# Attention beside a projection: V's first half turned sooner, a head's end in two steps

## The chip, the cores and the metric

The kernel runs on one core of one Trainium2 chip. The metric is the device time of one execution in microseconds. Five engines work side by side, each through its own instructions in the order in which the program lists them: TensorE (PE; its weight loads are shown as PEld), VectorE (DVE), ScalarE (ACT), GpSimd (POOL) and SyncE (SP), which here issues the transfers. An instruction that waits for a semaphore holds up all that stand behind it on its engine.

## The reference

One layer of a hybrid decoder on a sequence of 1024 tokens of width 2048, in float32. Cut to what matters here:

```python
proj = x @ w_in        # split: q, k, v, g_att (8 heads x 128 each), fg, conv and pool parts
cum = cumsum(log_sigmoid(fg + b_f))            # per head
logits = q @ k.T * 128 ** -0.5 + cum[q] - cum[k]      # causal: k <= q
y_att = softmax(logits) @ v * silu(g_att)
y = concat([y_att, y_conv, y_pool])            # each with its own silu gate
x = layer_norm(2 ** 0.25 * x + y @ w_out)
```

## The kernel before

A float32 product is made as three matmuls of a high and a low half (`mm3`): each operand is split by ACT, which casts the high half (L121), and DVE, which subtracts to get the low half (L122). Weights go through this under the names wr (as loaded) and wh (split), tiles of the softmax under t and pt, V under v, Q and K under qk.

The program has a first and a second pass over the input projection and then the output projection. In the second pass, 28 pairs of column blocks are projected in turn (8 `mm3` per block half and product); all that isn't projection runs beside it. It is put into slots of a queue: `at(slot, step)` adds a step some slots ahead, and every third `mm3` of the projection calls `tick()`, which takes the next slot and runs its steps. So a slot lasts about 2 to 2.6 us.

`attention(h, ...)` puts one head into these slots. Its 1024 queries are treated as two halves, n=0 (4 blocks of 128 keys) and n=1 (8 blocks), all tiles being keys x queries: `scores(n, j)` in slots 3 to 6 and 7 to 14; `find_top(n)` behind them, the maximum over the keys; `shift` (adds the negated maximum, L759), `probs` (exponential, on ACT L765), `parts` (the split into pt) and `values` (the product with V into the bank o) at slot e0 + j and one to three later, with e0 = 12 and 20; `turn_v(n)` transposes one half of V (PE, L675) and splits it; `invert(n)` makes the reciprocals of the row sums; `finish(n)` weights o with the gate (L797), multiplies by the reciprocals (L798), and stores the result. Behind `finish(1)`, `sums_of_y` loads, adds and stores sums of the results for the output projection (POOL and SP). A maximum or a row sum goes from one row to all 128 partitions through DRAM: `to_all` transposes a small tile on DVE (L745), writes it (m_dram) and reads it back to all partitions (the tile mb). Both the shift and L798 wait for such an mb.

What sets the order is not the slots alone. The steps are traced slot by slot, which gives each instruction its rank; a list scheduler then lays the instructions of each engine by rank and by when its model of the chip takes their inputs to be ready, and what it makes is the fixed order of the engine. The shift alone is held to the order of tracing: `keep_in_program_order` pins it behind the DVE instruction that was traced last before it. Buffers come from rings by tag: `gate` (tiles pa and pb, tag "pc", 7 buffers) is the gate that L797 and L798 overwrite with the result, and its buffer serves a later pair of blocks once the stores and `sums_of_y` have read it.

Of the kernel before, what the change touches and what calls it, by code (L numbers as in the profile page):

```python
# [36 lines left out]
ALU = mybir.AluOpType  # L37
# [8 lines left out]
H = S // 2  # L46
# [27 lines left out]
def layer(ctx: ExitStack, tc: tile.TileContext, xt, x, wp, wf, b_f, conv_w, pool_w, pool_scale,  # L74
          w_out, ln_g, ln_b, out):
    nc = tc.nc
# [31 lines left out]
    def hl(name, tag):  # L108
        return tile_of([P, 2, H], F32R, name, tag)
# [7 lines left out]
    def bank(tag):  # L117
        return ps.tile([P, 512], F32, tag=tag, bufs=4, name=nm(tag))

    def split(hi, lo, src):  # L120
        nc.scalar.copy(hi, src)  # L121
        nc.vector.tensor_tensor(lo, src, hi.bitcast(F32), ALU.subtract)  # L122
# [43 lines left out]
    def at(slot, step):  # L166

        while len(side) <= slot:
            side.append([])
        side[slot].append(step)  # L170
# [481 lines left out]
    def store_y(e, y, n):  # L652
        nc.sync.dma_start(y_dram[e, n], y[:, n * H : n * H + H])
# [13 lines left out]
    def attention(h, qs, ks, vt, gate):  # L667
        t, pt, v, o, top, down, total = {}, {}, {}, {}, {}, {}, {}

        def turn_v(n):  # L670
            def go():
                acc, th = bank("aux"), hl("v", "v")
                for a in range(4):
                    c = (n * 4 + a) * P
                    nc.tensor.transpose(acc[:, a * P : a * P + P], vt[:, c : c + P], ident)  # L675
                split(th[:, 0], th[:, 1], acc)
                v[n] = th
            return go
# [4 lines left out]
        def scores(n, j):  # L683
            def go():
                tj, c0 = half("t", "t"), first(n, j)
                t[n, j] = tj
                cw = min(c0, 256)
                if cw < c0:
                    nc.gpsimd.memset(tj[:, cw:c0], 0.0)
                acc = bank("aux")  # L690
                js = slice(j % 4 * P, j % 4 * P + P)
                kj = ks[j // 4]
                mm3(acc[:, cw:], kj[:, 0, js], kj[:, 1, js], qs[n][:, 0, cw:], qs[n][:, 1, cw:], True, True)
                ck = ncum[:, h, j : j + 1]
                plain = c0
                if j >= 4 * n:
                    plain = c0 + P
                    nc.vector.scalar_tensor_tensor(tj[:, c0:plain], acc[:, c0:plain], ck, mask, ALU.add, ALU.add)
                if plain < H:
                    nc.scalar.activation(tj[:, plain:H], acc[:, plain:], AF.Identity, bias=ck)  # L700
                if j:
                    fold_max(n, j, acc, ck, plain)
            return go
# [47 lines left out]
        def find_top(n):  # L751
            def go():
                down[n] = to_all(across(top[n], ALU.max), h * 4 + n)
            return go

        def shift(n, j):
            def go():
                tj, c0 = t[n, j], first(n, j)
                tc.keep_in_program_order(nc.vector.tensor_tensor(tj[:, c0:], tj[:, c0:], down[n][:, c0:], ALU.add))  # L759
            return go  # L760

        def probs(n, j):
            def go():
                tj, c0 = t[n, j], first(n, j)
                nc.scalar.activation(tj[:, c0:], tj[:, c0:], AF.Exp)  # L765
                if j:
                    fold(total, n, j, ALU.add, nc.gpsimd)
            return go

        def parts(n, j):  # L770
            def go():
                cw, th = min(first(n, j), 256), hl("pt", "pt")
                split(th[:, 0, cw:], th[:, 1, cw:], t[n, j][:, cw:])
                pt[n, j] = th
            return go

        def values(n, j):
            def go():
                if j == 0:
                    o[n] = bank("aux")  # L780
                cw = min(first(n, j), 256)
                js = slice(j % 4 * P, j % 4 * P + P)
                vj, th = v[j // 4], pt.pop((n, j))
                mm3(o[n][:, cw:], vj[:, 0, js], vj[:, 1, js], th[:, 0, cw:], th[:, 1, cw:], j == 0, j == 4 * n + 3)
            return go

        def invert(n):
            def go():
                w = across(total[n], ALU.add)
                nc.vector.reciprocal(w[:, :16], w[:, :16])  # L790
                total[n] = to_all(w, h * 4 + 2 + n)
            return go

        def finish(n):
            def go():
                y = gate[:, n * H : n * H + H]
                nc.vector.tensor_tensor(y, o[n], y, ALU.mult)  # L797
                nc.vector.tensor_tensor(y, y, total[n], ALU.mult)  # L798
                store_y(h, gate, n)
                if n:  # L800
                    at(1, sums_of_y(h, gate))
            return go

        for n, s0, e0 in ((0, 3, 12), (1, 7, 20)):
            js = 4 * n + 4
            for j in range(js):
                at(s0 + j, scores(n, j))
                at(e0 + j, shift(n, j))
                at(e0 + j + 1, probs(n, j))
            for j in range(js):  # L810
                at(e0 + j + 2, parts(n, j))
                at(e0 + j + 3, values(n, j))
            at(s0 + js, find_top(n))
            at((4, 9)[n], turn_v(n))
            at(e0 + js + 2, invert(n))
            at(e0 + js + 7, finish(n))


    def pool_steps(g, u, gate):
# [55 lines left out]
    def sums_of_y(k, y):  # L875
        def go():
            a21, s3 = half("a21", "m"), half("s3y", "m")
            nc.sync.dma_start(a21, y_dram[KH + k, 1])
            nc.sync.dma_start(s3, sy_dram[2, k])
            nc.gpsimd.tensor_tensor(s3, y[:, H:], s3, ALU.subtract)  # L880
            nc.sync.dma_start(sy_dram[1, k], s3)
            nc.gpsimd.tensor_tensor(a21, y[:, H:], a21, ALU.add)
            nc.sync.dma_start(sy_dram[0, k], a21)
            nc.gpsimd.tensor_tensor(y[:, :H], y[:, :H], s3, ALU.subtract)
            nc.sync.dma_start(sy_dram[3, k], y[:, :H])
        return go
# [48 lines left out]
    def use(role, g, a, b):  # L935
        if role == "vg":
            held[g] = a, b
        elif role == "qk":
            attention(g, *held.pop(("qk", g)), *held.pop(g))
        elif role == "pool":  # L940
            pool_steps(g, b, silu(a))
        elif role == "conv":
            held["conv"] = conv_steps(g, a, b)
        else:
            conv_gate(g, held.pop("conv"), a, b)
# [340 lines left out]
```

## Time and profile before

| | |
|---|---|
| median of 3 runs | 1631.89 us (1631.51 to 1632.08) |
| the profiled execution | 1629.22 us |
| its span, first to last instruction | 1627.5 us |
| granted TensorE clock, mean | 0.989 |
| busy: PE / PEld / DVE / ACT / POOL | 95% / 77% / 69% / 43% / 23% |
| first start of L798, last start | 750.3 us, 1360.5 us |
| heads 0 to 7 begin (first transpose of V) | 701, 781, 864, 951, 1037, 1128, 1201, 1276 us |

In a row of the timeline the columns are the start in us, the duration in us, the engine, the line, the operation, the tile written and the tiles read, the shape, and how many instructions the row holds; in square brackets, the engine's idle time before it and what ended that. A row of the waits holds the engine, line and tile that waited, what it waited for, the total in us, how often, and the longest.

### The profile page before, as it was taken

To read this page: it belongs to the slowest core of one execution; us is meant where nothing else is said; L and a number is where in the kernel's file an instruction comes from. 1 tells how busy PE (TensorE), PEld (TensorE's weight loads), DVE (VectorE), ACT (ScalarE), POOL (GpSimd) and SP (SyncE) were. 2 spreads that over 40 slices of the span, in tenths; PEclk is the share of its full clock that TensorE was granted. 3 is DMA by queue.
4 is the path that set the end of the run, shared out by engine and by line. 5 is a ranking of instruction groups with operands and counts; after the bars stand their busy time and mean duration, and the time that the engine had idled before them with its cause. 6 is when DMAs were issued, how large, how long until landed. Compare 5 with 4: busy or idle time off the path is not lost. (4 is left out here: it accounts for less than half of the span.)

```text
span 1627.5 us, 20130 instructions
## 1 busy us (share of the span) xinstructions
PE 1553.6 (95%) x6812; PEld 1254.3 (77%) x6812; DVE 1129.3 (69%) x1659; ACT 691.9 (43%) x1238; POOL 381.5 (23%) x303
## 2 busy tenths in 40 slices
PE   8999999999999999999999999999988998999986
PEld 6887888778787787788878777867766777788775
DVE  6754676666665656378787868577779875566797
ACT  4421221211121225566665656575666553444420
POOL 0232232222222220012232323343326322100000
PEclk9999999999999999999999999999999999999998
DMA  8756988887878667534545454535344445657572
GB/s 253 263 205 210 323 292 296 304 305 255 289 266 293 241 241 253 212 133 157 183 154 185 149 181 156 172 126 196 132 146 161 153 140 205 193 174 228 193 233 104
DMA packets 156807, 339.92 MB, mean 209 GB/s; under 512 B 17952, under 2 KB 27040, under 8 KB 156704
## 3 DMA queue, kind: packets, MB, share of 16 engines
q1 hardware_dynamic: 156704, 338.64, 61.2%
q8 instruction: 53, 0.87, 0.2%
q14 instruction: 50, 0.41, 0.1%
HBM read 247.28 MB, written 91.29 MB: 208 GB/s over the span
## 5 line engine op out<-in xcount | busy, mean ns | idle before, releaser
L122 DVE TENSOR_TENSOR wh<-wr,wh 128x512 fp32r<-128x512 f32 x264 | 199.4, 761 | 92.4 <-ACT wh L121 91.8
L121 ACT CAST wop<-wb 128x1024 fp32r<-128x1024 f32 x76 | 80.0, 1053 | 319.3 <-PE aux L129 139.2
L121 ACT CAST wh<-wr 128x512 fp32r<-128x512 f32 x264 | 161.5, 618 | 83.6 <-PE acc L130 27.9
L128 PE MATMUL acc<-x,wh 128*128 128x512 f32 x448 | 178.6, 399 | 3.3 <-ACT wh L121 3.3
L130 PE MATMUL acc<-x,wh 128*128 128x512 f32 x448 | 178.0, 397 | 3.4 <-DVE wh L122 3.4
L130 PE MATMUL aux<-xs,wop 128*128 128x512 f32 x448 | 175.5, 392 | 3.5 <-DVE wop L122 3.4
L129 PE MATMUL acc<-x,wh 128*128 128x512 f32 x448 | 176.3, 394 | 0.0
L128 PE MATMUL aux<-xs,wop 128*128 128x512 f32 x448 | 174.6, 390 | 0.0
L129 PE MATMUL aux<-xs,wop 128*128 128x512 f32 x448 | 174.4, 389 | 0.0
L122 DVE TENSOR_TENSOR wop<-wb,wop 128x1024 fp32r<-128x1024 f32 x76 | 102.7, 1352 | 27.1 <-ACT wop L121 27.0
L130 PEld LDWEIGHTS acc<-x,wh 128*128 128x128 f32 x448 | 84.7, 189 | 28.6 <-DVE wh L122 10.7
L130 PEld LDWEIGHTS aux<-xs,wop 128*128 128x128 f32 x448 | 84.1, 188 | 25.2 <-DVE wop L122 7.6
L128 PEld LDWEIGHTS acc<-x,wh 128*128 128x128 f32 x448 | 84.9, 190 | 22.5 <-ACT wh L121 7.2
L129 PEld LDWEIGHTS aux<-xs,wop 128*128 128x128 f32 x448 | 84.1, 188 | 17.7
L128 PEld LDWEIGHTS aux<-xs,wop 128*128 128x128 f32 x448 | 84.1, 188 | 17.5
L129 PEld LDWEIGHTS acc<-x,wh 128*128 128x128 f32 x448 | 85.0, 190 | 15.7
L130 PE MATMUL acc<-xs,wh 128*128 128x512 f32 x224 | 87.8, 392 | 3.4 <-DVE wh L122 3.4
L130 PE MATMUL acc<-xs,wop 128*128 128x512 f32 x224 | 88.0, 393 | 2.5 <-DVE wop L122 2.5
L122 DVE TENSOR_TENSOR pt<-t,pt 128x512 fp32r<-128x512 f32 (+1 forms) x96 | 84.5, 893 | 6.5 <-ACT pt L121 6.3
L128 PE MATMUL acc<-xs,wh 128*128 128x512 f32 x224 | 88.2, 394 | 0.0
L129 PE MATMUL acc<-xs,wh 128*128 128x512 f32 x224 | 87.4, 390 | 0.0
L128 PE MATMUL acc<-xs,wop 128*128 128x512 f32 x224 | 87.3, 390 | 0.0
(272 smaller groups left out, 3607.3 us busy)
## 6 DMA issues: line engine op xcount, KB each, us to landing
wb<-wp SPq DMA_DIRECT2D x116, 512.0 KB, 5.8
wr<-wp SPq DMA_DIRECT2D x112, 256.0 KB, 2.9
wo<-w_out SPq DMA_DIRECT2D x64, 256.0 KB, 6.0
o_dram<-wo SPq DMA_DIRECT2D x64, 256.0 KB, 4.5
wr<-o_dram SPq DMA_DIRECT2D x64, 256.0 KB, 2.8
t_dram<-wb SPq DMA_DIRECT2D x28, 512.0 KB, 5.8
a_dram<-ca SPq DMA_DIRECT2D x28, 512.0 KB, 3.8
b_dram<-cb SPq DMA_DIRECT2D x28, 512.0 KB, 4.6
```

The lines of the kernel that those rows point to most:

```text
L121: nc.scalar.copy(hi, src)
L122: nc.vector.tensor_tensor(lo, src, hi.bitcast(F32), ALU.subtract)
L128: nc.tensor.matmul(acc, wh, xh, start=start, stop=False, **more)
L129: nc.tensor.matmul(acc, wh, xl, start=False, stop=False, **more)
L130: nc.tensor.matmul(acc, wl, xh, start=False, stop=stop, **more)
```

## The change

`turn_v(0)` moves from slot 4 to slot 1, ahead of the scores. `finish` is cut in two: `weigh(n)`, the product with the gate, stands in slot e0 + js + 5 (21 and 33) instead of 23 and 35, and `finish(n)`, the product with the reciprocal sums and all behind it, in slot e0 + js + 9 (25 and 37).

```diff
+        def weigh(n):
+            def go():
+                y = gate[:, n * H : n * H + H]
+                nc.vector.tensor_tensor(y, o[n], y, ALU.mult)
+            return go
+
         def finish(n):
             def go():
                 y = gate[:, n * H : n * H + H]
-                nc.vector.tensor_tensor(y, o[n], y, ALU.mult)
                 nc.vector.tensor_tensor(y, y, total[n], ALU.mult)
                 store_y(h, gate, n)
                 if n:
...
             at(s0 + js, find_top(n))
-            at((4, 9)[n], turn_v(n))
+            at((1, 9)[n], turn_v(n))
             at(e0 + js + 2, invert(n))
-            at(e0 + js + 7, finish(n))
+            at(e0 + js + 5, weigh(n))
+            at(e0 + js + 9, finish(n))
```

The new lines move the later lines of the file: L798 becomes L803, and those behind it are 5 or 6 higher. The numbers at the ends of names differ between the two programs by the order in which tiles are made.

DVE at the end of head 2's top half (tiles pb_6159 the gate and result, mb_7164 the maximum of the bottom half, mb_7245 the reciprocal sums of the top half), before:

```order
L797 TENSOR_TENSOR pb_6159<-aux_7142,pb_6159 128x512
L736 TENSOR_REDUCE part_7230<-mt_7229 128x16
L122 TENSOR_TENSOR wh_7273<-wr_7215,wh_7273 128x512
L759 TENSOR_TENSOR t_6939<-t_6939,mb_7164 128x512
L759 TENSOR_TENSOR t_6963<-t_6963,mb_7164 128x512
...
L122 TENSOR_TENSOR wh_7324<-wr_7276,wh_7324 128x512
L798 TENSOR_TENSOR pb_6159<-pb_6159,mb_7245 128x512
L759 TENSOR_TENSOR t_7012<-t_7012,mb_7164 128x512
```

and of the change:

```order
L797 TENSOR_TENSOR pb_6159<-aux_7142,pb_6159 128x512
L736 TENSOR_REDUCE part_7230<-mt_7229 128x16
L759 TENSOR_TENSOR t_6963<-t_6963,mb_7164 128x512
L122 TENSOR_TENSOR wh_7273<-wr_7215,wh_7273 128x512
L759 TENSOR_TENSOR t_6929<-t_6929,mb_7164 128x512
...
L122 TENSOR_TENSOR wh_7325<-wr_7276,wh_7325 128x512
L759 TENSOR_TENSOR t_7012<-t_7012,mb_7164 128x512
L803 TENSOR_TENSOR pb_6159<-pb_6159,mb_7245 128x512
```

The shift of key block 1 (t_6963), which waits for the maximum, moved ahead of the split of a weight (wh_7273) and of the shift of block 0; the product with the reciprocal sums moved one shift later. Heads 1 and 3 read alike.

DVE at the end of head 2's bottom half (mb_7519 its reciprocal sums), before:

```order
L122 TENSOR_TENSOR wh_7532<-wr_7458,wh_7532 128x512
L797 TENSOR_TENSOR pb_6159<-aux_7341,pb_6159 128x512
L798 TENSOR_TENSOR pb_6159<-pb_6159,mb_7519 128x512
L122 TENSOR_TENSOR wh_7553<-wr_7489,wh_7553 128x512
L122 TENSOR_TENSOR wh_7573<-wr_7535,wh_7573 128x512
```

and of the change:

```order
L122 TENSOR_TENSOR wh_7532<-wr_7458,wh_7532 128x512
L797 TENSOR_TENSOR pb_6159<-aux_7339,pb_6159 128x512
L803 TENSOR_TENSOR pb_6159<-pb_6159,mb_7519 128x512
L122 TENSOR_TENSOR wh_7553<-wr_7489,wh_7553 128x512
L122 TENSOR_TENSOR wh_7582<-wr_7535,wh_7582 128x512
```

Nothing moved here, though the two products were traced four slots apart.

DVE at the end of head 5's top half (pb_8538 the gate, mb_9599 the maximum of the bottom half, mb_9696 the reciprocal sums of the top half, w_1674_9683 the row sum on its way), before:

```order
L797 TENSOR_TENSOR pb_8538<-aux_9577,pb_8538 128x512
L739 TENSOR_REDUCE w_1674_9683<-quads_9682 32x16
...
L122 TENSOR_TENSOR wh_9723<-wr_9666,wh_9723 128x512
L759 TENSOR_TENSOR t_9375<-t_9375,mb_9599 128x512
L759 TENSOR_TENSOR t_9400<-t_9400,mb_9599 128x512
L122 TENSOR_TENSOR wh_9746<-wr_9704,wh_9746 128x512
L759 TENSOR_TENSOR t_9418<-t_9418,mb_9599 128x512
L798 TENSOR_TENSOR pb_8538<-pb_8538,mb_9696 128x512
L759 TENSOR_TENSOR t_9449<-t_9449,mb_9599 128x512
L122 TENSOR_TENSOR pt_9764<-t_9375,pt_9764 128x512
```

and of the change:

```order
L797 TENSOR_TENSOR pb_8538<-aux_9577,pb_8538 128x512
L759 TENSOR_TENSOR t_9400<-t_9400,mb_9599 128x512
L739 TENSOR_REDUCE w_1674_9683<-quads_9682 32x16
...
L122 TENSOR_TENSOR wh_9723<-wr_9666,wh_9723 128x512
L759 TENSOR_TENSOR t_9365<-t_9365,mb_9599 128x512
...
L122 TENSOR_TENSOR pt_9765<-t_9365,pt_9765 128x512
...
L759 TENSOR_TENSOR t_9449<-t_9449,mb_9599 128x512
L803 TENSOR_TENSOR pb_8538<-pb_8538,mb_9696 128x512
```

The product with the reciprocal sums moved behind the split of pt (and behind a split of weights, left out here); the shift of block 1 moved up, directly behind the product with the gate and ahead of the fold of the row sum.

On SP, the store of the result and what `sums_of_y` loads and stores stand behind the next head's first maximum (its write to DRAM and its broadcast) and some loads of weights; so does the load of the pair that takes over the buffer of the gate. On ACT, in head 4, the silu of such a pair's tile stands between two exponentials, with a table load on either side.

## The prediction

> **What bounds the kernel now.** I read the page first, then the waits, then the row-by-row timeline of each head. The page:
>
> ```profile
> PE 1553.6 (95%) x6812; PEld 1254.3 (77%) x6812; DVE 1129.3 (69%) x1659; ACT 691.9 (43%) x1238; POOL 381.5 (23%) x303
> ```
>
> PE is the bound: 95% busy over a span of 1627.5 us, and the change adds and removes no matmul of a product (four transposes per head are only spread). So its whole effect is in the idle gaps of PE, and a microsecond on another engine counts where a gap ends on it. The waits that the change aims at are these:
>
> ```profile
> DVE pb L798 <- DMA mb<-m_dram: 30.1, 11, 5.9
> DVE t L759 <- DMA mb<-m_dram: 15.1, 6, 4.6
> ```
>
> L798 multiplies by the reciprocal row sums; 30.1 us of DVE idling stand in front of it, in 11 of its 16 runs. L759 adds the negated row maximum and waits for the same kind of broadcast. Both block all that stands behind them on DVE, the low halves of weights (wh, L122) above all. What such a wait costs PE is read head by head (heads 0 to 7, each with a top half n=0 and a bottom half n=1):
>
> ```profile
> 942.96 0.69 DVE L798 TENSOR_TENSOR pb<-pb,mb 128x512 f32<-128x512 f32 x1 [5.91 <-DMA mb<-m_dram]
> 944.31 0.50 PE L130 MATMUL acc<-x,wh 128*128 128x512 f32 x1 [1.35 <-DVE wh L122]
> 1183.44 0.69 DVE L798 TENSOR_TENSOR pb<-pb,mb 128x512 f32<-128x512 f32 x1 [3.56 <-DMA mb<-m_dram]
> 1185.39 0.50 PE L129 MATMUL aux<-pt,v 128*128 128x512 f32 x1 [2.21 <-DVE pt L122]
> 1187.70 0.50 PE L130 MATMUL acc<-x,wh 128*128 128x512 f32 x1 [0.19 <-DVE wh L122]
> 1211.98 0.69 DVE L798 TENSOR_TENSOR pb<-pb,mb 128x512 f32<-128x512 f32 x1 [2.37 <-DMA mb<-m_dram]
> 1218.26 0.76 PE L128 MATMUL aux<-qk,qk 128*128 128x512 f32 x1 [3.08 <-DVE m L725]
> ```
>
> Only three of the waits reach PE at once: 1.35 us in head 2, 2.40 (2.21 and 0.19) in head 5's top half, and part of 3.08 at head 5's end. That is 6.8 us at most out of 30.1.
>
> **The later product (finish).** By the order of instructions in the changed program, the bottom half's two products still stand back to back in heads 0 to 5 and 7, so the waits of 5.91 and 2.37 us stay: nothing for these. In the top halves of heads 0 to 4 the product goes one row later where it didn't wait: nothing. In head 5's top half it goes behind the splits that PE waited for; the 2.40 us go: **-2.4**. What comes in their place there is below.
>
> **The weighting (weigh) and what it pulls along.** Each shift (L759) is pinned behind the instruction traced before it on DVE. Since the weighting stands in slot 21, shift(1,1) is now pinned right behind L797, and with it the wait for the bottom half's maximum. In heads 1 to 3 a weight split (wh) stood ahead of that wait and now stands behind it. Heads 2, 1, 0 and 3 before:
>
> ```profile
> 905.53 0.68 DVE L122 TENSOR_TENSOR wh<-wr,wh 128x512 fp32r<-128x512 f32 x1
> 910.78 1.29 DVE L759 TENSOR_TENSOR t<-t,mb 128x512 f32<-128x512 f32 x2 [4.57 <-DMA mb<-m_dram]
> 908.77 0.39 PE L130 MATMUL acc<-x,wh 128*128 128x512 f32 x1
> 909.00 0.39 PE L128 MATMUL acc<-x,wh 128*128 128x512 f32 x1
> 912.70 0.50 PE L128 MATMUL acc<-x,wh 128*128 128x512 f32 x1 [1.49 <-ACT wh L121]
> 914.99 3.45 DVE L122 TENSOR_TENSOR pt<-t,pt 128x512 fp32r<-128x512 f32 x2
> 916.80 0.50 PE L129 MATMUL aux<-pt,v 128*128 128x512 f32 x1 [1.29 <-DVE pt L122]
> 825.14 1.29 DVE L759 TENSOR_TENSOR t<-t,mb 128x512 f32<-128x512 f32 x2 [2.84 <-DMA mb<-m_dram]
> 824.86 0.39 PE L130 MATMUL acc<-x,wh 128*128 128x512 f32 x1
> 831.17 0.50 PE L129 MATMUL aux<-pt,v 128*128 128x512 f32 x1 [1.28 <-DVE pt L122]
> 742.11 1.29 DVE L759 TENSOR_TENSOR t<-t,mb 128x512 f32<-128x512 f32 x2 [1.30 <-DMA mb<-m_dram]
> 998.26 1.29 DVE L759 TENSOR_TENSOR t<-t,mb 128x512 f32<-128x512 f32 x2 [4.19 <-DMA mb<-m_dram]
> 996.62 0.39 PE L130 MATMUL acc<-x,wh 128*128 128x512 f32 x1
> 1004.28 0.51 PE L129 MATMUL aux<-pt,v 128*128 128x512 f32 x1 [1.27 <-DVE pt L122]
> ```
>
> The L130 rows are the first use of that low half. In head 2 it will be ready at 910.78 + 0.6 (shift, pitch of a back-to-back pair) + 0.6 (split) = 912.0, and PE wants it at 908.77: a new stall of 3.2 us. In head 1: 826.3 against 824.86, 1.5 us; in head 3: 999.5 against 996.62, 2.8 us. Together 7.5. Most of it is taken back, since PE stalls soon after for a pt split whose chain starts at the same broadcast: that stall ends when the chain does, which is later by the one split now in it, 0.6 us, and by two matmuls (0.23 us from one start to the next, 908.77 to 909.00) that now stand behind the waiting one. So the net is 0.6 + 0.46 = 1.06 us a head: **+3.2**. Bounds: 1.8 (0.6 each) to 7.5. I take the first, as the later stall's own chain is in the trace. In head 0 the wait was the shortest of the four, 1.30 us: little, **+0.2**.
>
> A stall has a second price. The granted clock (PEclk) in two stretches of 3.50 us:
>
> ```profile
> core 0: us, PE busy (x) PEld busy (x) DVE busy (x) ACT busy (x) POOL busy (x), PEclk, DMA share, GB/s
> 1071.40:1074.90 3.50, 1.03 (x6) 0.65 (x5) 3.50 (x5) 2.12 (x5) 3.50 (x6) 1.00 0.26 75
> 1074.90:1078.40 3.50, 3.50 (x11) 2.81 (x11) 3.43 (x8) 0.00 (x0) 3.50 (x3) 0.51 0.26 75
> ```
>
> After 3.50 us with PE busy for 1.03, the next 3.50 ran at 0.51 of the clock: 0.49 x 3.50 = 1.7 us lost. The new stalls of 3.2 and 2.8 us are of that size; the pt stall hides part, and where the stretches begin isn't known: 0 to 3.4, I take **+1.0**. The Trainium skill ("TensorE: Matmul & The Clock Gate", "HAM oscillation — how this bites in real kernels") warns only of PE idling over about 3.4 us; by it neither stall would halve the clock, and the sum would be 1.0 lower. The trace differs: its longest gap there was 2.46 us, and the clock fell.
>
> Another move there pays. The first pt split of a head waited for ACT and now goes behind other rows, and a weight split comes sooner:
>
> ```profile
> 892.90 0.50 PE L130 MATMUL acc<-x,wh 128*128 128x512 f32 x1 [0.27 <-DVE wh L122]
> 980.77 0.50 PE L130 MATMUL acc<-x,wh 128*128 128x512 f32 x1 [0.30 <-DVE wh L122]
> 1157.13 0.50 PE L130 MATMUL acc<-x,wh 128*128 128x512 f32 x1 [0.40 <-DVE wh L122]
> ```
>
> These three go: **-1.0**.
>
> **Head 5's top half, the other side.** Shift(1,1) stood behind a weight split; now it is ahead of it:
>
> ```profile
> 1176.73 0.64 DVE L122 TENSOR_TENSOR wh<-wr,wh 128x512 fp32r<-128x512 f32 x1
> 1177.39 1.29 DVE L759 TENSOR_TENSOR t<-t,mb 128x512 f32<-128x512 f32 x2
> ```
>
> The maximum lands by 1177.39, where L759 began without a wait. Behind it will now stand the row sum's fold, a q/k part (0.7) and the split: 1177.4 + 0.6 + 0.25 + 0.7 + 0.25 + 0.6 = 1179.8, against an end at 1177.37 that PE used at once. That is a stall of up to 2.3 us; and the row sum's broadcast, some 4 us later, keeps DVE about 0.5 us at the moved product: **+2.8**, bounds 0 (the maximum came well before 1177) and 4.5 (with half a clock).
>
> **The gate's buffer, freed later; V turned sooner.** The store of y and the loads and stores of the sums after it go behind the next maximum on SP's queue, and with them the load of a later pair into the freed buffer. In head 4 ACT already idles for one:
>
> ```profile
> 1058.98 0.63 ACT L649 ACTIVATE pb<-pb 128x512 f32<-128x512 f32 x1 [5.67 <-DMA pb<-b_dram]
> 1062.64 1.28 ACT L765 ACT_TABLE_LOAD   x1
> 1065.60 0.50 PE L128 MATMUL acc<-x,wh 128*128 128x512 f32 x1 [0.70 <-ACT wh L121]
> ```
>
> The silu of that half now comes between two exponentials, which brings one pair of table loads more, 2 x 1.28 = 2.6 us of ACT ahead of a weight cast; on the other hand ACT no longer idles those 5.67 us, and the 0.70 goes. -1.0 to +2.6: **+0.8**, the middle. V's transposes and split come sooner in a place where DVE idles for weight casts; the first scores come some 30 matmuls later but no row of the later scores moves: nothing, unless head 6 shows it:
>
> ```profile
> 1281.47 0.50 PE L129 MATMUL aux<-pt,v 128*128 128x512 f32 x1 [1.41 <-DVE pt L122]
> 1287.99 0.39 PE L128 MATMUL aux<-pt,v 128*128 128x256 f32 x1 [0.40 <-ACT pt L121]
> 1301.64 0.50 PE L128 MATMUL acc<-wh,xy 128*128 128x512 f32 x1 [1.05 <-ACT c L1075]
> 1257.97 1.29 DVE L759 TENSOR_TENSOR t<-t,mb 128x512 f32<-128x512 f32 x2 [1.84 <-DMA mb<-m_dram]
> 1261.72 0.96 PE L128 MATMUL acc<-wh,xy 128*128 128x512 f32 x3 [3.27 <-ACT wh L121]
> ```
>
> There the rows about 1270 to 1300 are shuffled: the late pt split comes four rows sooner, and the product before 1301 has a weight split and a fold ahead of it. 1.41 + 0.40 + half of 1.05: **-2.3**, bounds -2.9 and 0. The wait at 1257.97 also goes ahead of a split there, but PE idles until 1261.72 for an ACT cast that doesn't move: nothing. Head 7 and the end: the same move, less room: **+0.3**.
>
> **Sum:** -2.4 + 3.2 + 0.2 + 1.0 - 1.0 + 2.8 + 0.8 - 2.3 + 0.3 = **+2.6 us**. The profiled execution took 1629.22 us (1.7 outside its span), 2.7 below the median of the runs, 1631.89. So 1631.8 for such an execution, and **1634.5** for the median. 0.2% is 3.3 us, about what a measurement tells from no change; the forecast lies just inside.
>
> **The rivals.**
> *Faster, the waits go and nothing replaces them* (0.20). The late broadcasts in heads 1 to 3 come sooner as well, or PE has enough queued, and head 5's maximum is there in time: -2.4 - 1.0 - 2.3 = -5.7, 1626.2. For it: head 5's 3.56-us wait is truly gone. Against it: the 2.84, 4.57 and 4.19 us at L759 start from DVE's own transposes, which don't come sooner.
> *Slower, the maximum's wait takes the sum's place* (0.16). Shift(1,1) with its wait ahead of the weights costs its whole 7.5 us in heads 1 to 3, and both halves of clock, 3.4, since the pt chain slips with PE: the sum with 7.5 and 3.4 for 3.2 and 1.0 is +9.3, 1641.2. It decides from the point where the pt split is late by more than the 0.6 us of one split. For it: pt splits there took 1.7 us each (3.45 for two), so a row more in that chain can cost more than 0.6. Against it: that chain hangs on the same broadcast.
> *It doesn't do what it says* (0.16). Most products don't move at all, and what moves meets idle time of DVE (69% busy): 1631.9.
> *My forecast* (0.48): the trade of small stalls, 1631.5 to 1638.
>
> **How the numbers follow.** Faster: the first rival and a sliver of the forecast, 0.22. Slower: the second, and the upper part of the forecast, from 1635.2 on, 0.21: 0.37. Same: 0.16 and 0.25: 0.41. The range reaches towards both outer cases until about a tenth is left out on each side, 1627 to 1640; the forecast's own is 1631.5 to 1638.
>
> **What would show it.** L798's (new line L803's) wait for mb should fall from 30.1 to about 25 us, with the bottom halves' as they are; L759's should grow from 15.1 to 18 or more, in the same heads. New PE gaps behind DVE wh near 824, 908 and 996, and the pt gaps at 831 and 1004 not gone. In head 5, 2.21 gone and a gap near 1177 instead. A gap-free 820 to 1010, or L759's wait grown without gaps, would prove me wrong to the fast side; more stretches of half clock than before to the slow side.

## The result: 0.8% slower

The changed kernel took 1646.16 us (median of 3 runs, 1644.3 to 1648.14) against 1631.89 before: a ratio of 1.0082, 95% interval 1.0066 to 1.0099. Two repetitions beside new runs of the kernel before gave 1.0064 (1.0048 to 1.0081) and 1.0073 (1.0052 to 1.0094). So the loss is some 12 to 14 us. The forecast was 1634.5, within 1627 to 1640.

The page of the changed kernel, profiled at 1646.16 us (span 1644.4 us):

```profile
PE 1557.5 (95%) x6812; PEld 1256.3 (76%) x6812; DVE 1121.5 (68%) x1659; ACT 696.7 (42%) x1240; POOL 369.8 (22%) x303
```

PE does the same matmuls and is 3.9 us longer busy than in the first profile of before, but only 1.2 us longer than in a second one (1556.3 us); the rest are gaps. Its waits, first of the kernel before, then of the changed one with two waits of DVE (engine, tile and line that waited, what for, us in total, times, longest):

```profile
PE aux L129 <- DVE pt L122: 12.7, 10, 2.5
PE acc L128 <- ACT wh L121: 8.2, 5, 3.3
PE acc L130 <- DVE wh L122: 6.7, 10, 1.4
```

```profile
PE acc L130 <- DVE wh L122: 13.4, 10, 2.6
PE aux L129 <- DVE pt L122: 10.7, 10, 4.2
PE acc L128 <- ACT wh L121: 4.0, 4, 2.0
DVE pb L803 <- DMA mb<-m_dram: 29.0, 9, 5.9
DVE t L759 <- DMA mb<-m_dram: 26.5, 9, 4.3
```

The wait of the product with the reciprocal sums, which was to fall to about 25 us, is nearly as it was (30.1 us then, 29.0 now). The wait of the shift for the maximum grew from 15.1 to 26.5 us, and what PE waits for low halves of weights doubled.

To place the loss, I took from each trace the starts of the same matmuls of the projections and of the output product (their order is the same in all kernels) and counted how much longer each kernel took from one to the next than the first profile of the kernel before. The columns are parts of that profile, in us from its start:

| kernel | first pass, 6 to 648 | heads 0-3, 648 to 1035 | head 4, to 1142 | head 5, to 1223 | head 6, to 1310 | head 7, to 1466 | output, to 1563 |
|---|---|---|---|---|---|---|---|
| before, second profile | +4.4 | -3.9 | +0.5 | -1.3 | +0.5 | -0.5 | +2.6 |
| changed | +5.5 | -1.8 | +5.4 | +2.7 | -0.9 | +2.3 | +3.8 |
| changed, second | +5.5 | -1.3 | +6.3 | +3.2 | -0.7 | +1.9 | +2.6 |
| changed, third | +1.2 | -2.4 | +5.7 | +1.9 | -1.5 | +5.0 | +2.7 |

The first row is the warning: two profiles of the same kernel differ by 4 us in the first pass (whose instructions the change leaves as they are) and by 4 again in heads 0 to 3. Against the mean of the two profiles of before, the changed kernel loses 10.9 us from 648 to 1466, on the mean of its three: some 5.5 in head 4, 3.2 in head 5, 3.3 in head 7, nothing that can be told in heads 0 to 3 (the two profiles of before differ by 3.9 there; over all the kernels below, this stretch took 385.3 us on the mean of the eleven profiles with the pinned shift and 385.0 in the six without), and gains 1.3 in head 6. The rest, in the first pass and the output product, is no more than one profile differs from another.

### The profile page after: what moved, and what is told of

Its sections match the earlier page's. It is cut to its first block, busy times and chain, and to the rows that moved or that the text cites. A ratio compares the mean times of both kernels' runs of the same rounds, so it can differ in the third digit from the quotient of the medians.

```text
span 1644.4 us, 20123 instructions
## 1 busy us (share of the span) xinstructions
PE 1557.5 (95%) x6812; PEld 1256.3 (76%) x6812; DVE 1121.5 (68%) x1659; ACT 696.7 (42%) x1240; POOL 369.8 (22%) x303
## 5 line engine op out<-in xcount | busy, mean ns | idle before, releaser
L122 DVE TENSOR_TENSOR wh<-wr,wh 128x512 fp32r<-128x512 f32 x264 | 199.5, 762 | 98.5 <-ACT wh L121 97.9
L122 DVE TENSOR_TENSOR wop<-wb,wop 128x1024 fp32r<-128x1024 f32 x76 | 107.2, 1410 | 27.9 <-ACT wop L121 27.8
L759 DVE TENSOR_TENSOR t<-t,mb 128x512 f32<-128x512 f32 (+2 forms) x96 | 71.3, 743 | 26.5 <-DMA mb<-m_dram 26.5
```

## The experiments

All were made beside runs of the kernel before on the same chip; ratios are to those. Two ratios whose intervals are 0.3% wide can be told apart when they differ by about 0.25% (4 us) or more.

### What one profile and one repetition are worth

The kernel before, a second time:

> The kernel before, profiled a second time, to see how far one profile differs from another where nothing is changed. Four profiles of kernels whose first 600 us are the same row by row reached the matmul at 308 us of the first profile 1.9 to 5.5 us later. Theory (that first profile was a lucky one): 2 to 5 us later here too, and 0 to 5 us of difference in the output projection after 1466 us; between 648 and 1466 us within 1.5 us.

1631.83 us against 1632.57, ratio 1.0002 (0.9987 to 1.0017); the profile started the second pass 4.4 us later, and took 3.9 us less in heads 0 to 3, where 1.5 was expected at most. So single gaps may be read from a profile, but a sum of 4 us over hundreds of microseconds may not.

The changed kernel again, twice:

> The changed kernel once more, beside the kernel before on the same chip. In the first profile of it 5.5 us of the loss lay in the first 620 us, where its instructions are the same as before, row by row. Theory A (those 5.5 us come with the run or the chip, not with the change): the loss here is 8 to 11 us, and the first pass starts the second within 2 us of the kernel before. Rival B (the changed program itself makes the first pass slower): 13 to 16 us, with the same 5 us before 620 us.

> The changed kernel again, as the measure for the three that differ from it at one place each, on the same chip. 10 to 14 us above the kernel before. Its first pass (up to 648 us of the first profile), which has the same rows as before: if the 5.5 us of its first two profiles are chance, 0 to 5 this time; if they belong to the program, 5.5 again.

1644.07 us against 1632.08 and 1642.70 against 1630.26: 12.0 and 12.4 us. The first pass took 5.5 us more and then 1.2 us more than in the first profile of before. I take it for chance; it was not settled further.

### The three edits apart

V turned sooner, and nothing else:

```diff
-            at((4, 9)[n], turn_v(n))
+            at((1, 9)[n], turn_v(n))
```

> The kernel before with one edit: the first half of V is turned in slot 1. No wait is moved and the order of SP's transfers for maxima, sums and stores is that of before. Theory A (the loss comes from the later product and the shift that is pinned behind the weighting): 0 to -3 us against before, the gain in head 6 if there is one. Rival B (the earlier transposes and split of V cost PE or DVE time in each head): +3 us or more, with new gaps of PE within 10 us of the heads' beginnings.

1629.75 us against 1632.08, ratio 0.9984 (0.9969 to 0.9998). Because this would be the version that beats both kernels, it ran again:

> The version with V turned sooner and nothing else once more, on another chip or at another time: 1 to 4 us faster than the kernel before if the first result (2.3 us, interval 0.02% to 0.31%) was right; within 1 us of it if it was chance.

1631.05 against 1630.69, ratio 1.0000 (0.9987 to 1.0014). The loss does not come from this edit; a gain isn't established. One place gained all the same: both of its profiles took less in head 4 than the first profile of before, by 3.5 and 3.7 us, and ran none of it at half clock, where the two of before ran 3.4 and 6.8 us. So the 5.5 us that the changed kernel lost in head 4 come on top of a gain that it had no more, some 9 us counted from this version.

The weighting in a step of its own (`weigh` as in the change, its line taken out of `finish`), and nothing else:

```diff
+            at(e0 + js + 5, weigh(n))
             at(e0 + js + 7, finish(n))
```

> The kernel before, with the weighting in its own step two slots sooner and nothing else: V is turned in slot 4, the product with the reciprocal sums stays in slots 23 and 35, and SP's order is that of before. It has the pin alone. Rival B (the pin costs 8 to 10 us by itself): 1640 to 1642. Theory A (the pin costs 2 to 4 us unless SP is late too): 1634 to 1636.

1636.29 against 1632.57, ratio 1.0026 (1.0009 to 1.0042): 3.7 us, just above what theory A named (1634 to 1636).

The other side: the changed kernel with the weighting traced behind the shifts of its slot, so that no shift is pinned to it; the two new lines stand behind the loop over n.

```diff
-            at(e0 + js + 5, weigh(n))
             at(e0 + js + 9, finish(n))
+        at(21, weigh(0))
+        at(33, weigh(1))
```

> The changed kernel, but the weighting is traced behind the shifts of its slot, so that the shift is no longer pinned behind it and the weight split stands ahead of the wait for the maximum again, as before the change. SP's order stays that of the changed kernel. Theory A (most of the loss comes from SP: the sums of y and the gate's buffer behind the next maximum; the pin costs 2 to 4 us, 2.6 of it in head 4): 2 to 4 us faster than the changed kernel; the extra pair of table loads in head 4 and the 4-us gap of PE in head 7 stay. Rival B (the pin is what costs): 8 us or more faster than the changed kernel, back within 3 us of the kernel before.

1634.27 against 1632.08, ratio 1.0014 (1.0002 to 1.0026), so some 8 to 10 us faster than the changed kernel: rival B. The wait of its shifts:

```profile
DVE t L759 <- DMA mb<-m_dram: 20.5, 7, 4.1
```

Seven of the nine waits are left, but in heads 0 to 4 and 6 a weight split now runs ahead of the wait; head 5's is gone. Head 4's gaps behind ACT and DVE were still there, and head 7's stall too, as theory A had it. So the pin costs 3.7 us when it is alone and 8 to 10 when the later product is there too: the two costs seem not to add, each is dearer beside the other. (The kernel with the pin alone turns V late and the others turn it sooner. That this makes the pin dear isn't likely, since the kernel below that has the pin and V turned sooner, but two of the later products back, costs only 2.8 us.) In its profile, the gain against the mean of the changed ones is 1.4 us in heads 0 to 3, 1.6 in head 4, 3.6 in head 5, 0.3 in head 6 and -1.1 in head 7. That is 6; the other 2 to 4 stand in parts whose rows are equal, within what two profiles differ.

### The later product and SP's queue

The changed kernel with the sums of y one slot sooner:

```diff
                 store_y(h, gate, n)
                 if n:
-                    at(1, sums_of_y(h, gate))
+                    at(0, sums_of_y(h, gate))
```

> The changed kernel, but the sums of y come in the slot right behind the later product, one slot sooner, so that SP takes their loads and stores ahead of the next head's maximum again. The pinned shift stays. Theory A (SP): the extra table loads in head 4 and the 4-us gap of PE in head 7 are gone, 7 to 10 us faster than the changed kernel, within 4 us of the kernel before. Rival B (the pin): within 2 us of the changed kernel, with the gaps behind the pinned shift in heads 1 to 4 as they are.

1642.10 against 1632.08, ratio 1.0056 (1.0041 to 1.0070): 2 us of gain at most, rival B by the time. Yet the profile showed what theory A named: head 4 at -2.4 us and head 7's stall gone. What came instead was 5.9 us in head 5 and a different order on SP in head 6. So this edit changed more than it was meant to, and says little on its own.

Together with the weighting unpinned:

> Both undone: the weighting is traced behind the shift of its slot, and the sums of y come one slot sooner; the later product and the V turned sooner stay. If the two costs add up (10 us for the pin and 2 for the sums, of the 12): about 1632, within 2 us of the kernel before. If they overlap, because SP's order alone costs little once DVE isn't held: as with the pin alone undone, 1634. If the later product has a price of its own: 1636 or more.

1633.85 against 1632.57, ratio 1.0011 (0.9995 to 1.0028). Not apart from the kernel before, nor from the unpinned kernel: without the pin, SP's order costs little or nothing that these runs can tell.

A cleaner cut: the pin stays, and the bottom half's product is put back into its old slot in heads 3 and 6 alone, the two whose late sums of y the profile had met in heads 4 and 7.

```diff
-            at(e0 + js + 9, finish(n))
+            at(e0 + js + (7 if (h, n) in ((3, 1), (6, 1)) else 9), finish(n))
```

> The changed kernel, but the later product of the bottom half of heads 3 and 6 alone is back in its old slot (35), so that the sums of y of these two heads stand on SP ahead of the next maximum. The pin stays in all heads, the later product in all others. Theory A (in the profiles the table loads in head 4 cost some 6 us and SP's block in head 7 some 4): 7 to 10 us faster than the changed kernel. Rival B (the pin is nearly all, since undoing it alone gave 10 us and bringing the sums forward only 2): 0 to 3 us faster.

1635.36 against 1632.57, ratio 1.0020 (1.0005 to 1.0034): 7 to 10 us faster than the changed kernel by its three ratios, theory A. Two places out of sixteen hold most of the loss, with the pin in place in all eight heads.

Head 6 alone (slot 35 for (6, 1) only):

> The changed kernel, but the later product of the bottom half of head 6 alone is back in slot 35. On SP the loads and stores of its sums of y then stand ahead of head 7's maxima and row sums. Theory (SP, held by the sums, sends head 7's row sum 5 us late, and PE stalls 4.2 us for it and then runs at half clock): the gap of PE near 1351 is gone and the time falls by 4 to 6 us. Rival (the loss is given back right after, since 2.8 us come back within the next 100 us): 1 to 3 us.

1641.54 against 1630.26, ratio 1.0072 (1.0051 to 1.0092): 1 us, the rival. The stall was there and went. On SP in the changed kernel, then in this one (start, duration, line, transfer; rows of weight loads left out):

```profile
1336.72 0.43 SPq L885 DMA_DIRECT2D s3y<-sy_dram  x1
...
1342.83 0.32 SPq L889 DMA_DIRECT2D sy_dram<-a  x1
1343.24 0.38 SPq L746 DMA_DIRECT2D m_dram<-w32t  x1
...
1345.07 0.32 SPq L748 DMA_DIRECT2D mb<-m_dram  x1
```

```profile
1337.32 0.32 SPq L746 DMA_DIRECT2D m_dram<-w32t  x1
1339.61 0.32 SPq L748 DMA_DIRECT2D mb<-m_dram  x1
```

The row sum of head 7 was transposed (L745) at 1338.21 in the changed kernel, and sent at 1343.24, 5 us later, because the store of the sum `a` stood ahead of it on SP and waited for POOL, which itself had waited for the load of `a`. Behind it on DVE and PE:

```profile
1338.21 0.20 DVE L745 STREAM_TRANSPOSE w32t<-w 32x32 f32<-32x32 f32 x1
1349.21 0.69 DVE L803 TENSOR_TENSOR pb<-pb,mb 128x512 f32<-128x512 f32 x1 [5.86 <-DMA mb<-m_dram]
1350.29 1.28 DVE L122 TENSOR_TENSOR pt<-t,pt 128x512 fp32r<-128x512 f32 x2
1351.03 0.80 PE L129 MATMUL aux<-pt,v 128*128 128x512 f32 x1 [4.19 <-DVE pt L122]
```

That is the largest single loss of the change, 5.7 to 6.0 us at its place in the first two profiles (in the first, 4.19 us of gap, the rest half clock) and 3.3 in the third. But without it PE met other waits: 1.38 us for an eviction of the output product at 1365.29, where the changed kernel's profile has 0.56 at 1371.61, and, ahead of the place, 1.89 at 1337.03. The time says 1 us net, with an interval of at least 3 us to either side.

Head 3 alone:

> The changed kernel, but the later product of the bottom half of head 3 alone is back in slot 35: its sums of y go ahead of head 4's maximum on SP, the buffer of its gate is free sooner, and the extra table loads are gone. Undoing it in heads 3 and 6 gave 9 us, in head 6 alone 1.2. If the places add up: 7 to 8 us faster than the changed kernel, about 1636 to 1638, with 5 to 6 us of it in head 4. If head 4's loss is given back later, as head 7's was: 0 to 3 us.

1638.05 against 1630.69, ratio 1.0049 (1.0031 to 1.0066): 2.5 to 4 us by the two repetitions' ratios, between the two, with 6 us of gain in head 4 of its profile. Apart the two places gave some 1 and 3 us, together 7 to 10. What is missing, some 5 us, is about as much as the intervals of these ratios leave open together, so that the places don't add up is likely and not shown.

### Head 4: tables or transfers

In head 4 the later product had several consequences at once: late transfers, two more table loads on ACT, and a late maximum. ACT in the changed kernel:

```profile
1060.87 1.11 ACT L528 COPY acc<-pa 128x512 f32<-128x512 f32 x2 [3.21 <-DMA pa<-a_dram]
...
1067.45 0.58 ACT L528 COPY acc<-pb 128x512 f32<-128x512 f32 x1
1068.05 1.28 ACT L649 ACT_TABLE_LOAD   x1
1069.35 0.63 ACT L649 ACTIVATE pb<-pb 128x512 f32<-128x512 f32 x1
1070.00 1.28 ACT L765 ACT_TABLE_LOAD   x1
...
1072.44 0.63 ACT L121 CAST wh<-wr 128x512 fp32r<-128x512 f32 x1
```

and PE:

```profile
1073.12 0.50 PE L128 MATMUL acc<-x,wh 128*128 128x512 f32 x1 [1.96 <-ACT wh L121]
1075.61 0.79 PE L130 MATMUL acc<-x,wh 128*128 128x512 f32 x1 [1.75 <-DVE wh L122]
1093.86 0.50 PE L130 MATMUL acc<-x,wh 128*128 128x512 f32 x1 [2.59 <-DVE wh L122]
```

The weight cast stands behind the silu and both table loads. The split behind it took 2.38 us, since POOL was at work beside it (see the last section). In the kernel before the same split took 2.12 us, beside POOL as well, but PE's gap behind it was 0.58.

The third gap takes the pin and the later product together: the shift stands ahead of the split of a weight, and the maximum that it waits for came late. SP, first in the kernel before, then in the changed one (the write of the maximum, L746, and its broadcast, L748; in the first a load of pb between them is left out):

```profile
1079.82 0.32 SPq L746 DMA_DIRECT2D m_dram<-w32t  x1
1081.76 0.32 SPq L748 DMA_DIRECT2D mb<-m_dram  x1
```

```profile
1084.50 0.32 SPq L746 DMA_DIRECT2D m_dram<-w32t  x1
1088.19 0.32 SPq L187 DMA_DIRECT2D wr<-t_dram  x1
1088.56 0.43 SPq L748 DMA_DIRECT2D mb<-m_dram  x1
```

In the changed kernel the broadcast stands behind a load of weights that waits 3.3 us for a split on DVE, and leaves 4.06 us after the write, for 1.94 before; the shift waited 2.57 us, where it did not wait before. With the pin alone the broadcast left after 1.95 us, the shift waited 0.20 us and PE had no gap there. With the later product and no pin the broadcast left after 4.07 us and the shift waited 2.36 us, but the weight split was done and that gap was gone (two of some 1 us behind ACT came near it). With head 3's product back, SP's order is that of before, and the gap isn't there.

To price the tables, first alone, added to the kernel with heads 3 and 6 back:

```diff
                 nc.scalar.activation(tj[:, c0:], tj[:, c0:], AF.Exp)
+                if (h, n, j) == (4, 0, 0):
+                    extra = small.tile([P, 1], F32, tag="extra", bufs=1, name=nm("extra"))
+                    tc.keep_in_program_order(nc.scalar.activation(extra, tj[:, c0:c0 + 1], AF.Silu))
```

> The kernel with heads 3 and 6 back, whose only added rows are one silu of a column of one element per partition behind the first exponential of head 4 (into a scratch tile that nothing reads) and the two table loads that it brings. Nothing else moves on any engine. It prices the extra pair of table loads by itself: 2 x 1.28 us of ACT. If the pair is what costs head 4 its 6 us: 4 to 7 us slower than with heads 3 and 6 back (1635.4 there), so 1639 to 1642, with the gaps of PE near 1073 behind an ACT weight cast. If it is the late load and not the tables: within 1.5 us of 1635.4.

1638.13 against 1630.26, ratio 1.0046 (1.0025 to 1.0066). By the time it is 0.26% above the kernel with heads 3 and 6 back, at the edge of what can be told; by the profile head 4 took as long as in that kernel (both within 0.1 us of before). The cast came 6.1 us behind the start of the first exponential instead of 3.8, and PE's gap was one of 1.47 in place of three small ones (0.51, 0.27, 0.57). Nothing settled.

Then the reverse, the changed kernel less these two table loads:

```diff
-            silu(cb[:, H:])
+            (silu(cb[:, H:]) if g != 5 else nc.scalar.copy(cb[:, H:], cb[:, H:]))
```

> The changed kernel, with the silu of head 5's second half of gates replaced by a copy (so that half of head 5's gates isn't right): this takes the two table loads in head 4 away and moves nothing else on any engine. If the tables cost head 4 its 6 us: 4 to 6 us faster than the changed kernel, 1637 to 1639, without the PE gaps of 1.96 and 1.75 us near 1073. If it is the late transfers and the order around them: within 1.5 us of the changed kernel (1642.7 to 1646), the gaps as they were or elsewhere in the same head.

1642.73 against 1630.69, ratio 1.0070 (1.0052 to 1.0089): the changed kernel's time. In the profile, head 4 still lost 2.5 us against 5.4 to 6.3. Its gaps there:

```profile
1069.90 0.50 PE L130 MATMUL acc<-x,wh 128*128 128x512 f32 x1 [1.76 <-DVE wh L122]
1071.65 0.44 PE L128 MATMUL aux<-pt,v 128*128 128x384 f32 x1 [0.78 <-ACT pt L121]
1073.23 0.69 PE L129 MATMUL aux<-pt,v 128*128 128x384 f32 x1 [0.66 <-DVE pt L122]
1088.17 0.50 PE L130 MATMUL acc<-x,wh 128*128 128x512 f32 x1 [1.04 <-DVE wh L122]
```

The 1.96 behind ACT is gone, the 1.75 behind DVE is not. So the tables explain about half of head 4's loss at its place, in one profile, and none that the time shows. What the later transfers do by themselves was not isolated in a run.

### The pin in one head

The changed kernel, unpinned in head 5 alone:

```diff
-            at(e0 + js + 5, weigh(n))
+            if h != 5:
+                at(e0 + js + 5, weigh(n))
             at(e0 + js + 9, finish(n))
+        if h == 5:
+            at(21, weigh(0))
+            at(33, weigh(1))
```

> The changed kernel, but in head 5 alone the weighting is traced behind the shift of its slot, so that the weight split stands ahead of the wait for the maximum. Only rows of head 5 differ. The forecast had +2.8 us there, and -2.4 for the product that moved. If that is so: 2 to 4 us faster than the changed kernel, and in this head the wait of the product before the pt split comes back. If the pin costs its 10 us elsewhere or all over: within 1.5 us.

1641.20 against 1630.26, ratio 1.0066 (1.0043 to 1.0090): 1.5 us, below what can be told. In its profile head 5 took 3.4 us less than in the changed kernel's three on the mean. DVE in head 5 of the changed kernel, then of this one:

```profile
1182.69 0.68 DVE L797 TENSOR_TENSOR pb<-aux,pb 128x512 f32<-128x512 f32 x1
1185.37 0.69 DVE L759 TENSOR_TENSOR t<-t,mb 128x512 f32<-128x512 f32 x1 [2.00 <-DMA mb<-m_dram]
...
1186.91 0.62 DVE L122 TENSOR_TENSOR wh<-wr,wh 128x512 fp32r<-128x512 f32 x1
1187.58 0.80 PE L130 MATMUL acc<-x,wh 128*128 128x512 f32 x1 [2.01 <-DVE wh L122]
```

```profile
1185.12 1.29 DVE L759 TENSOR_TENSOR t<-t,mb 128x512 f32<-128x512 f32 x2 [0.20 <-DMA mb<-m_dram]
1189.57 1.11 DVE L803 TENSOR_TENSOR pb<-pb,mb 128x512 f32<-128x512 f32 x1 [1.96 <-DMA mb<-m_dram]
1191.81 0.50 PE L129 MATMUL aux<-pt,v 128*128 128x512 f32 x1 [1.09 <-DVE pt L122]
```

The new gap of 2.01 us goes with the pin, and half of the old one of 2.21 comes back.

Head 5's loss stands elsewhere: at its end, where PE waits for DVE ahead of the next head's scores (before: 3.08 us at 1218.26, 2.52 in the second profile). A weight split on that way in the kernel before, then the changed kernel, with POOL beside it:

```profile
1216.85 0.69 DVE L122 TENSOR_TENSOR wh<-wr,wh 128x512 fp32r<-128x512 f32 x1 [0.64 <-ACT wh L121]
```

```profile
1225.96 1.89 POOL L835 TENSOR_TENSOR sum<-pb 128x1023 f32<-128x1023 f32 x1
1226.29 2.10 DVE L122 TENSOR_TENSOR wh<-wr,wh 128x512 fp32r<-128x512 f32 x1 [0.64 <-ACT wh L121]
1229.11 0.79 PE L128 MATMUL aux<-qk,qk 128*128 128x512 f32 x1 [5.31 <-DVE m L725]
```

The gap is 5.31, 5.20 and 5.35 us in the changed kernel's three profiles. It is 3.85 to 5.75 us in all twelve profiles of kernels whose head 5 has the later product, and 2.06 to 3.08 in the five without it. Before, POOL's sums of y came first there (1224.13) and the sum for the pool part after them (1229.25); with sums of y later, that sum runs while DVE splits the weight. Unpinning head 5 brings the gap to 4.04 us only, and with heads 3 and 6 back it is 5.75. No run puts head 5's product back alone.

### What the runs settle, and what not

Shown: the weighting's pin and the later product of the bottom half (in heads 3 and 6) each carry a large part. Undoing the pin everywhere takes the ratio from 1.0064 to 1.0014; undoing the product in the two heads takes it to 1.0020. Either is enough to bring back most of the 12 us, and each alone costs a third of them or less (3.7 us for the weighting by itself, 2.2 for the product without the pin, with V turned sooner; each with an interval of 2 to 3 us to either side). Shown too: the places, by gaps that appear and vanish with their cause, and in head 4 how the two meet: the later product makes the maximum late, and the pin puts a weight split behind it. Not settled: whether that is all of what they cost more together than apart, and how the single places, of which each timed 1 to 4 us, make up the whole. What head 5's later product is worth by itself, a part of head 4's loss, and the first pass, stay open as well.

## Why the prediction was wrong

The direction of its mean was right (+2.6), the size was not, and it lay within "no change". The terms that failed are three: head 4, in the sum with +0.8, lost 5.5 us; the end of head 5, in it with nothing, where the gap grew by some 2.5 us; and head 7, in it with +0.3, lost 3.3 us. In all three the later product changed an order on SP or POOL that the working had followed to the gate's buffer alone. By its steps:

- **The later product.** Right where it said "nothing": the waits behind the bottom halves stayed (5.16 us in head 2, for 5.91). Right in head 5's top half: DVE's wait of 3.56 us and the gap of 2.21 us are gone. But the sum of these waits, forecast to fall to about 25 us, is 29.0: in head 7's top half the wait grew from 2.52 to 5.86 us.
- **Heads 1 to 3, +3.2 and half a clock +1.0.** Right in the mechanism, and the first term came out at its places: each new gap and what was left of the pt gap, less the pt gap before, make 0.9, 1.2 and 1.2 us in this profile. The gaps stand where they were forecast, and the pt gaps shrank:

```profile
832.84 0.50 PE L130 MATMUL acc<-x,wh 128*128 128x512 f32 x1 [1.29 <-DVE wh L122]
838.10 0.51 PE L129 MATMUL aux<-pt,v 128*128 128x512 f32 x1 [0.87 <-DVE pt L122]
917.02 0.50 PE L130 MATMUL acc<-x,wh 128*128 128x512 f32 x1 [1.56 <-DVE wh L122]
922.29 0.50 PE L129 MATMUL aux<-pt,v 128*128 128x512 f32 x1 [0.89 <-DVE pt L122]
1001.94 0.50 PE L130 MATMUL acc<-x,wh 128*128 128x512 f32 x1 [1.60 <-DVE wh L122]
1007.20 0.50 PE L129 MATMUL aux<-pt,v 128*128 128x512 f32 x1 [0.88 <-DVE pt L122]
```

  1.29, 1.56 and 1.60 us where 1.5, 3.2 and 2.8 were worked out: the broadcast does not run on PE's clock, and came 1.7 us nearer to PE's need in head 2 (PE 6.6 us later there than before, the maximum 4.9). No half clock came. The small gaps (0.27 and 0.30 us) went, but in their places PE waited 0.48, 0.63 and 0.57 us for ACT's cast of pt, so the -1.0 was not had. Heads 0 to 3 still lost nothing that can be told. The ACT gaps of 1.49 and 1.13 us, which the sum left out, are gone in the changed kernel; but in the second profile of before they are 0.35 us and nothing, so they are no steady gain.
- **Head 5, +2.8 against -2.4 and -0.4.** The gap near 1177 came, 2.01 us for "up to 2.3", for the 2.21 that went. Half a clock stands behind it, as behind the stall in head 7:

```profile
core 0: us, PE busy (x) PEld busy (x) DVE busy (x) ACT busy (x) POOL busy (x), PEclk, DMA share, GB/s
1184.00:1187.40 3.40, 1.43 (x6) 0.53 (x4) 2.03 (x5) 1.94 (x5) 0.00 (x0) 0.97 0.35 111
1187.50:1190.90 3.40, 3.32 (x8) 2.67 (x9) 3.35 (x6) 3.20 (x7) 2.07 (x3) 0.54 0.44 148
1347.60:1351.00 3.40, 0.00 (x0) 0.00 (x0) 1.79 (x4) 0.59 (x2) 0.00 (x0) 1.00 0.54 186
1351.10:1354.50 3.40, 3.40 (x8) 2.75 (x9) 3.26 (x6) 2.51 (x5) 0.91 (x1) 0.51 0.39 117
```

  The stretch of half clock behind 1187 is no loss by itself: the second profile of before has one there too, and both have one near 1163 that the changed kernel hasn't. In all, head 5 had 6.8 us at half clock in both profiles of before and 10.2, 10.2 and 6.8 in those of the changed kernel. Head 5 lost 3.2 us where the terms summed to nothing, and most of it is the gap at its end, 5.31 us for 3.08 and 2.52. The forecast had shown the 3.08 and left it as it was. The Trainium skill ("TensorE: Matmul & The Clock Gate", "HAM oscillation — how this bites in real kernels") warns of gaps above some 3.4 us. The 4.19 us of head 7 fits it; the 2.01 us of head 5, with PE busy for 1.43 of 3.40 us, was followed by 0.54 of the clock as well, so here too the trace goes further than the page.
- **Head 4, +0.8 "the middle" of -1.0 to +2.6.** This failed. 5.5 us were lost. The table loads were named and stand where the text put them, but the cast behind them was priced as if it had slack, the slow DVE split behind it (1.75 us of gap) was not in the sum, and the pin was not looked for in head 4, where the shift had not waited before and now, with the broadcast late on SP, left a gap of 2.59 us. The upper bound was the table loads' own duration, when the queue behind them had a price too.
- **Head 7, +0.3 "the same move, less room".** This failed too: 3.3 us on the mean, 5.7 to 6.0 at its place. The text told that SP's loads, stores and sums go behind the next maximum, and costed the buffer of the gate; it did not ask what then stands behind the sums. That was head 7's row sum, held on SP by a store that waits for POOL.
- **Head 6, -2.3.** Of the right sign: -1.3, hardly more than profiles differ.
- **The rivals.** The slower rival put its price in heads 1 to 3, where nothing was lost. Its mechanism, a maximum's wait ahead of the weights, was at work in heads 4 and 5. That the pin and the later product would make each other dearer was in none of the cases; the terms were added as if each stood alone.

## What to carry to other kernels

When a step is moved on an engine that only issues transfers, follow what comes to stand behind it there, not only what it was moved behind: a store that waits for a slow engine holds every small transfer after it, and a row sum that left 5 us late for that cost PE a stall of 4 us. An instruction pinned to the one traced before it inherits that one's new place, with its wait; trace a moved step behind the pinned ones of its slot. And don't count on terms of a few microseconds to add up on engines that feed each other: two edits that cost some 4 and 2 us by themselves cost 12 together.

## What the runs showed of the hardware that I had not expected

Two profiles of one kernel can differ by 4 us in a stretch where nothing is changed, and in either direction (+4.4 in the first pass, -3.9 in the next 387 us), while the medians of many runs agree within 0.05%: 1631.83 and 1632.57 us. A gap at its place is a better witness than a difference of offsets. And a loss of PE that is 6 us long at its place (head 7) was worth some 1 us of the time, since PE met the next waits sooner without it.

POOL can hold DVE. Of the 480 splits of 128x512 on L122 in the first profile of before, 414 took some 0.7 us and 55 over 1.1 us. Each of these 55 ran beside a row of POOL and ended 0.55 us after that row's end, as the 2.10 us of head 5's end do (POOL's row ended at 1227.85, the split at 1228.39).

The stretches of half clock begin and end on a grid of 3.413 us in all 17 profiles. After each step of that grid in which PE was busy for under 1.5 us, the next ran at half clock; after one at full clock with more than 1.95 us busy, none did. So what a gap costs in clock depends on how it falls on the grid, and not on its length alone.
